# A two-layer diffusion backbone on one core: low parts of weights computed on POOL, modulation steps placed in other units

## The chip, the cores and the metric

The kernel runs on one core of a Trainium2 chip. The metric is the device time of one execution in microseconds (us); the median of 3 runs is 2028.29 us (2028.06 to 2028.62). Everything is float32, and the matmuls work on fp32r operands. The engines are TensorE (PE, with its weight loads as PEld), VectorE (DVE), ScalarE (ACT), GpSimd (POOL) and SyncE (SP), which issues most of the DMAs; POOL issues some.

## What is computed

Two layers over 256 latent tokens and 256 context tokens of width 1024. A vector of conditioning gives, per layer, nine modulation vectors of 1024 values for each of the two streams (`m`, from `w_ada`). A layer is a half-weighted SwiGLU FFN (hidden width 2816), a mixer with three branches (2-D Fourier, bidirectional retention, differential attention), and a second FFN. In the last layer only the latent stream goes on behind the mixer.

```python
m = (sc @ w_ada[l] + b_ada[l]).reshape(B, N_MOD, 1, D)
x = x + 0.5 * m[:, 2] * swiglu(modulate(rms_norm(x, norm_g[l, 0]), m[:, 0], m[:, 1]), w1[l, 0], w3[l, 0], w2[l, 0])
h = modulate(rms_norm(x, norm_g[l, 1]), m[:, 3], m[:, 4])
...
mixed = gf * (f_out @ wbf) + gr * (r_out @ wbr) + gd * (d_out @ wbd)   # gf, gr, gd: sigmoid(h @ w_gates)
x = x + m[:, 5] * (mixed @ wo)
x = x + 0.5 * m[:, 8] * swiglu(modulate(rms_norm(x, norm_g[l, 2]), m[:, 6], m[:, 7]), w1[l, 1], w3[l, 1], w2[l, 1])
```

## The kernel before

**Three products for one.** Every large product is computed as hi·hi + hi·lo + lo·hi: a weight block of 128 x 4 x 256 values is loaded (`wraw`), ACT casts it to fp32r (`whi`, line 330), and an engine subtracts (`wlo = wraw - whi`, line 331, in `split_act`). `split` takes the engine as an argument; the default is DVE. Only the first weights and the branch weights of the mixers name POOL.

**The stages.** There are four FFNs and two mixers, in the order first FFN, first mixer, second FFN (layer 0's other), third FFN (layer 1's first), second mixer, last FFN. The first three FFNs work on 512 columns (`ffn_both`), the last one on 256 (`ffn`). Each `ffn_both` runs one list of units through `pipeline`: four ordinary units, then sevens and downs. A seven (`seven`, seven units of 24 matmuls of 256 columns) computes the up and the gate product of 256 hidden channels with seven products of half-size blocks instead of eight; sums of weight blocks (`s1` to `s4`) and of quarters of the normed input (`Forms.fills`) feed it. A down unit (`down`, `chunk`) multiplies up to four 128-row blocks of `w2`, 24 matmuls of 512 columns. The list is two sevens, eight downs, four sevens, eight downs, three sevens, six downs; the last two channel blocks follow by themselves.

**What sets the order.** In `pipeline` PE, DVE and ACT take the order in which the program is written. Unit i's weights are prepared three units ahead (ACT's cast, then the low part), behind what unit i - 1 left to do at once (`now`: the residual of line 553, or the additions of line 771), and before its modulation steps and its matmuls. The modulation vectors are made in between on DVE: a vector is eight steps, and each step loads 512 KB of `w_ada` (SP) and adds it, scaled, to two accumulators (two instructions of line 242; 240 for the first step). A vector ends with eight small matmuls (line 258), a copy on DVE (263) and four transposes (266). Where the steps go is said by a unit's `cost`: `want` grows by cost times `scale`, which is steps over the sum of costs, and up to two steps are issued in front of the unit. Until the first eight are done the scale is at least 1, since the gate vector is needed for the residual.

```python
if i < len(units):
    want += units[i].cost * (max(scale, 1) if did < KD else scale)
    if units[i].cost:
        for _ in range(2):
            if did < min(total, int(want + 1e-6)) and not held[0] and step():
                did += 1
```

POOL and SP aren't bound to that order; POOL also issues the second half of the loads of `s1` and `s3` (line 737), which is added to the first half in flight and waits for it. The raw weights and the modulation loads share five buffers.

**The mixers.** The scheduler orders them. `merged` runs once for each branch: for each of four pairs of channel blocks two gate pieces of `w_in` (128x1024 each, `split` in line 1389), 24 matmuls each, and the branch's own product. The first two branches' merges are woven into the attention as fill, the third stands behind it. The first mixer works on 512 columns and makes three vectors, the second on 256 and makes one, during its third merge and output product.

Of the kernel before, what the change touches and what calls it, by code (L numbers as in the profile page):

```python
# [17 lines left out]
P = 128  # L18
# [61 lines left out]
def dit_kernel(ctx: ExitStack, tc: tile.TileContext, I: dict, out: bass.AP):  # L80
# [544 lines left out]

    def pipeline(units, fills, steps, total, made):

# [16 lines left out]
        with tc.manual_schedule(engines={eng.PE, eng.DVE, eng.Activation}):  # L644
            for i in range(len(units) + 1):
                prev = units[i - 1] if i else None
                if prev:
                    if prev.need is not None:
                        assert did >= prev.need, did
                        finish(True)  # L650
                    for f in prev.now:
                        f()
                while pi < min(len(units), i + 4):
                    while li < len(units) and (li <= pi or out + units[li].takes <= 3):
                        if units[li].load:
                            units[li].load()
                        out += units[li].takes
                        li += 1
                    units[pi].w = units[pi].prep()
                    out -= units[pi].gives  # L660
                    pi += 1
                if pi < len(units) and units[pi].first:
                    units[pi].first()
                for f in fills.get(i, ()):
                    f()
                finish()
                if prev:
                    for f in prev.end:
                        f()
                if i < len(units):  # L670
                    want += units[i].cost * (max(scale, 1) if did < KD else scale)
                    if units[i].cost:
                        for _ in range(2):

                            if did < min(total, int(want + 1e-6)) and not held[0] and step():
                                did += 1
                    units[i].mm(units[i].w)
# [4 lines left out]
    class Forms:  # L682


        def __init__(self, norm, spare, first):
# [9 lines left out]

            def whole(o, a, b):
                v.tensor_tensor(o, a.bitcast(F32), b.bitcast(F32), ALU.add)

            def neg(a, b):
                v.scalar_tensor_tensor(a, a, -1.0, b, op0=ALU.mult, op1=ALU.subtract)  # L700

            self.fills = {
                1: [lambda: whole(t[2], h22, l22), lambda: whole(t[0], h11, l11), lambda: whole(t[1], h12, l12)],
                2: [lambda: v.tensor_tensor(t[0], t[0], t[1], ALU.subtract),
                    lambda: v.tensor_tensor(t[1], t[2], t[1], ALU.subtract)],
                3: [lambda: split_act(z[0][:, 0], z[1][:, 0], t[0]), lambda: split_act(z[0][:, 2], z[1][:, 2], t[1])],
                4: [lambda: whole(t[1], h21, l21), lambda: neg(t[0], t[2]),
                    lambda: split_act(z[0][:, 1], z[1][:, 1], t[0])],
# [15 lines left out]
    def seven(fm, wa, wb, c0, fp, done, cost):  # L724
# [58 lines left out]
        def gate(h, by):  # L783
# [7 lines left out]
            Unit(part("c", fm.t1, True), whole("s1"), None, 0, 0, [keep("p5", "c")], cost=0),  # L791
            Unit(part("b", fm.t2), whole("s2"), None, 0, 1, [keep("w1", "b")], cost=1, first=summed("s2", "s1", "a11")),
            Unit(part("a", fm.b21, True), whole("a12"), raw("a12", wa, 1), 1, 0, [add("q1", "a")], [silu(0, "q1")], cost=cost),
# [6 lines left out]
    def ffn_both(l, f, norm, mods, then, first):  # L800
# [5 lines left out]
        with tc.tile_pool(name=f"ffn{l}{f}", bufs=1) as fp:  # L806
# [12 lines left out]

            def chunk(w, r, n, c0, acc, start, stop, xs, **more):  # L820
                x = {}
# [9 lines left out]

                return Unit(mm, lambda: split(x["w"], n, 2 * P), load, 1, 1, **more)

# [31 lines left out]
            def down(cg, r0, kt, last, need):  # L865
# [18 lines left out]
                for k in range(0, kt, 4):  # L884
                    n = min(4, kt - k)
                    more = {"cost": 0.25 * n}
                    if k + n == kt and need is None:
# [19 lines left out]
            for c0, c1 in ((2, 4), (4, 8), (8, 11)):  # L907
                g0 = 0 if c0 == 2 else c0
                for c in range(c0, c1):
                    units += seven(fm, w1, w3, c * 2 * P, fp, to(c - g0), 1 if first and c < 4 else 0.3)  # L910
                for cg in range(4 if c1 < KF // 2 else 3):
                    units += down(cg, 2 * g0, 2 * (c1 - g0), c1 == KF // 2, KD if first and g0 == 0 and cg < 2 else None)
            made = []
            with norm.done():
                pipeline(units, fm.fills, ada(mods, fp, made), KD * len(mods), made)
            for _ in to_residual(w2, 6, (g["hi"], g["lo"]), NTOK, gate, st, fp, weight_places, 16, then, (3,)):
# [105 lines left out]
    def mixer(l, nq, entry, mods, then):  # L1022
# [38 lines left out]
        with tc.tile_pool(name=f"mx{l}", bufs=1) as mp:  # L1061
# [319 lines left out]
            def merged(n, get, pool):  # L1381
# [4 lines left out]
                for d in range(0, KD, 2):  # L1386
                    acc = get("pg")
                    for c in range(2):
                        wt = split([rowsof(win, 4 * c, 4, O_GT + n * D + d * P, 256)], 4, 256)
                        for k in range(4):  # L1390
# [129 lines left out]
    entry = mixer_entry(0)  # L1520
    ffn_both(0, 0, after, [(0, m) for m in range(2, 5)], entry, True)
    load_mixer_consts()
# [3 lines left out]
    after = ffn_entry(0, 1, NTOK)  # L1526
    mixer(0, NTOK, entry, [(0, m) for m in (5, 6, 7)], after)
    load_bias(1)()
    entry = ffn_entry(1, 0, NTOK)
    ffn_both(0, 1, after, [(0, 8)] + [(1, m) for m in range(3)], entry, True)  # L1530
    after = mixer_entry(1)
    ffn_both(1, 0, entry, [(1, m) for m in range(3, 7)], after, False)
    entry = ffn_entry(1, 1, L)
    mixer(1, L, after, [(1, 7)], entry)
    ffn(1, 1, entry, [(1, 8)], Output())
# [22 lines left out]
```

## Time and profile before

| what | value |
|---|---|
| median of 3 runs | 2028.29 us (2028.06 to 2028.62) |
| profiled execution | 2025.39 us, span 2023.6 us |
| PE busy | 1931.0 us, 95% |
| PEld busy | 1729.6 us, 85% |
| DVE busy | 1599.2 us, 79% |
| ACT busy | 977.9 us, 48% |
| POOL busy | 129.4 us, 6% |
| mean granted clock of PE | 0.986 |

A busy PE is one with a matmul in its pipeline, so its idle time is what can be read from it. Stretches are given in us from the span's start: first FFN 46 to 393, first mixer to 816, second FFN to 1191, third to 1555, second mixer to 1837, last FFN to the end. A wait names the engine and line that came last.

### The profile page before, as it was taken

The numbers are of one execution on the slowest core, as the hardware profiler recorded it, in microseconds if no ns is written. First come the engines' busy times: TensorE is split into PE (matmuls) and PEld (weight loads), VectorE is DVE, ScalarE is ACT, GpSimd is POOL, SyncE is SP. The second block draws the span as 40 slices with busy tenths as digits, with TensorE's granted clock in tenths as the row PEclk, the third lists the DMA queues.
The fourth block names the chain that finished last, engine by engine and source line by source line (L and its number), as shares of the span: only waits on it lengthen the run. The fifth ranks groups of instructions, "written<-read, shape, count | busy, mean of one in ns | idle before, by whom it ended". The sixth has DMA issues, their size and how long they took to land. (4 is left out here: it accounts for less than half of the span.)

```text
span 2023.6 us, 32546 instructions
## 1 busy us (share of the span) xinstructions
PE 1931.0 (95%) x12959; PEld 1729.6 (85%) x12959; DVE 1599.2 (79%) x2365; ACT 977.9 (48%) x1487; POOL 129.4 (6%) x86
## 2 busy tenths in 40 slices
PE   7899999999999999989999999999999999889998
PEld 5789989897777678888998988889898988889998
DVE  6888868698788865797887878888788689898655
ACT  4433525464476434542543545345254768555444
POOL 2100100000000110110100000011000001110000
PEclk8999999999999999999999999999999999999999
DMA  9875854454322433665876465778644334475763
GB/s 318 211 222 157 221 170 121 137 174 132 107 65 87 162 109 119 153 171 182 215 213 166 125 159 154 209 186 233 177 141 117 107 91 144 125 248 178 238 193 110
DMA packets 283296, 331.24 MB, mean 164 GB/s; under 512 B 15664, under 2 KB 265096, under 8 KB 282888
## 3 DMA queue, kind: packets, MB, share of 16 engines
q1 hardware_dynamic: 254632, 300.84, 47.0%
q0 software_dynamic: 28512, 28.32, 9.4%
q8 instruction: 102, 1.67, 0.3%
q14 instruction: 50, 0.41, 0.1%
HBM read 325.97 MB, written 3.15 MB: 163 GB/s over the span
## 5 line engine op out<-in xcount | busy, mean ns | idle before, releaser
L330 ACT CAST whi<-wraw 128x1024 fp32r<-128x1024 f32 (+2 forms) x368 | 366.7, 1000 | 506.6 <-PE py L326 198.2
L331 DVE TENSOR_TENSOR wlo<-wraw,whi 128x1024 fp32r<-128x1024 f32 (+2 forms) x340 | 398.5, 1176 | 155.6 <-ACT whi L330 151.3
L242 DVE SCALAR_TENSOR_TENSOR aacc<-wada,cs,aacc 128x1024 f32<-128x1024 f32 x224 | 279.4, 1284 | 2.5 <-DMA wada<-w_ada 2.4
L763 PE MATMUL p<-hhi_f,whi 128*128 128x256 f32 x864 | 246.1, 285 | 23.5 <-DVE half L771 23.5
L763 PE MATMUL p<-hlo_f,whi 128*128 128x256 f32 x864 | 243.3, 282 | 0.0
L763 PE MATMUL p<-hhi_f,wlo 128*128 128x256 f32 x864 | 243.1, 281 | 0.0
L763 PE MATMUL p<-zone,whi 128*128 128x256 f32 x1296 | 230.9, 281 | 5.9 <-ACT half L768 5.2
L763 PEld LDWEIGHTS p<-zone,whi 128*128 128x128 f32 x1296 | 198.9, 190 | 7.8 <-ACT half L768 6.7
L325 PE MATMUL py<-ghi,whi 128*128 128x512 f32 x492 | 192.5, 391 | 0.7 <-DVE modT L268 0.7
L763 PEld LDWEIGHTS p<-hhi_f,whi 128*128 128x128 f32 x864 | 165.2, 191 | 31.8 <-DVE half L771 19.2
L327 PE MATMUL py<-ghi,wlo 128*128 128x512 f32 x492 | 191.5, 389 | 0.0
L326 PE MATMUL py<-glo,whi 128*128 128x512 f32 x492 | 191.4, 389 | 0.0
L763 PE MATMUL p<-zone,wlo 128*128 128x256 f32 x648 | 181.8, 281 | 0.0
L325 PE MATMUL p<-hhi_f,whi 128*128 128x256 f32 (+1 forms) x576 | 177.7, 309 | 2.3 <-DVE hhi_f L398 2.3
L327 PE MATMUL p<-hhi_f,wlo 128*128 128x256 f32 (+1 forms) x576 | 176.5, 307 | 3.0 <-DVE wlo L331 2.4
L326 PE MATMUL p<-hlo_f,whi 128*128 128x256 f32 (+1 forms) x576 | 177.0, 307 | 0.3
L763 PEld LDWEIGHTS p<-hhi_f,wlo 128*128 128x128 f32 x864 | 166.4, 193 | 0.0
L763 PEld LDWEIGHTS p<-hlo_f,whi 128*128 128x128 f32 x864 | 165.2, 191 | 0.3
L327 PE MATMUL pg<-hhi_m,wlo 128*128 128x512 f32 (+1 forms) x384 | 131.2, 342 | 5.8 <-DVE wlo L331 5.8
L325 PE MATMUL pg<-hhi_m,whi 128*128 128x512 f32 (+1 forms) x384 | 133.2, 347 | 3.5 <-ACT whi L330 2.5
L737 POOL DMA_DIRECT2D s<-ffn_w x54 | 72.2, 1337 | 905.3 <-DMA s<-ffn_w 412.8
L326 PE MATMUL pg<-hlo_m,whi 128*128 128x512 f32 (+1 forms) x384 | 130.1, 339 | 0.0
(367 smaller groups left out, 4447.1 us busy)
## 6 DMA issues: line engine op xcount, KB each, us to landing
wraw<-ffn_w SPq DMA_DIRECT2D x229, 512.0 KB, 4.4
wada<-w_ada SPq DMA_DIRECT2D x128, 512.0 KB, 4.1
wraw<-w_in SPq DMA_DIRECT2D x64, 512.0 KB, 3.6
s<-ffn_w SPq DMA_DIRECT2D x54, 512.0 KB, 5.3
s<-ffn_w POOLq DMA_DIRECT2D x54, 512.0 KB, 7.4
wraw<-w_out SPq DMA_DIRECT2D x16, 512.0 KB, 3.8
wada<-w_ada SPq DMA_DIRECT2D x30, 256.0 KB, 6.4
wraw<-w_in SPq DMA_DIRECT2D x16, 384.0 KB, 3.7
```

Of the source, the lines that this page charges most:

```text
L242: v.scalar_tensor_tensor(acc[:, t], w, cs[:, k, t:t + 1], acc[:, t], op0=ALU.mult, op1=ALU.add)
L325: te.matmul(o, a, xh, start=start, stop=False)
L326: te.matmul(o, a, xl, start=False, stop=False)
L327: te.matmul(o, b, xh, start=False, stop=stop)
L330: s.copy(hi, src)
L331: eng.tensor_tensor(lo, src, hi.bitcast(F32), ALU.subtract)
L737: gp.dma_start(t, rowsof(second[0], 4 * second[1], 4, c0, 2 * P), accum_op=ALU.add)
L763: te.matmul(om, wt[w][:, k, cm], form[f][:, k], start=(first and k == m == n == 0), stop=(k == 3 and m == 1 and n == 2), skip_group_check= ...
```

## The change

It names POOL for the low parts of the down units' weights and of gate pieces (all of them in the first mixer, the first of each pair in the second), and for two of the sums over quarters of the normed input. The cost of a full down unit goes from 1 to 1.6; of a seven's three paying units two go to 0 (from 0.3) and one from 1 to 0.6, but for the first two sevens of the first FFN. The rule of the first eight steps holds in the first FFN alone. The vectors are made one stage earlier: four in each of the first three FFNs, three in the first mixer, none in the second, one in the last FFN as before.

```diff
-    def pipeline(units, fills, steps, total, made):
+    def pipeline(units, fills, steps, total, made, first):
...
-                    want += units[i].cost * (max(scale, 1) if did < KD else scale)
+                    want += units[i].cost * (max(scale, 1) if first and did < KD else scale)
...
-            def whole(o, a, b):
-                v.tensor_tensor(o, a.bitcast(F32), b.bitcast(F32), ALU.add)
+            def whole(o, a, b, eng=v):
+                eng.tensor_tensor(o, a.bitcast(F32), b.bitcast(F32), ALU.add)
...
-                1: [lambda: whole(t[2], h22, l22), lambda: whole(t[0], h11, l11), lambda: whole(t[1], h12, l12)],
+                1: [lambda: whole(t[2], h22, l22, gp), lambda: whole(t[0], h11, l11), lambda: whole(t[1], h12, l12)],
...
-                4: [lambda: whole(t[1], h21, l21), lambda: neg(t[0], t[2]),
+                4: [lambda: whole(t[1], h21, l21, gp), lambda: neg(t[0], t[2]),
...
-            Unit(part("b", fm.t2), whole("s2"), None, 0, 1, [keep("w1", "b")], cost=1, first=summed("s2", "s1", "a11")),
+            Unit(part("b", fm.t2), whole("s2"), None, 0, 1, [keep("w1", "b")], cost=max(cost, 0.6), first=summed("s2", "s1", "a11")),
...
-            def chunk(w, r, n, c0, acc, start, stop, xs, **more):
+            def chunk(w, r, n, c0, acc, start, stop, xs, eng=v, **more):
...
-                return Unit(mm, lambda: split(x["w"], n, 2 * P), load, 1, 1, **more)
+                return Unit(mm, lambda: split(x["w"], n, 2 * P, eng=eng), load, 1, 1, **more)
...
-                    more = {"cost": 0.25 * n}
+                    more = {"cost": 0.4 * n, "eng": gp}
...
-                    units += seven(fm, w1, w3, c * 2 * P, fp, to(c - g0), 1 if first and c < 4 else 0.3)
+                    units += seven(fm, w1, w3, c * 2 * P, fp, to(c - g0), 1 if first and c < 4 else 0)
...
-                        wt = split([rowsof(win, 4 * c, 4, O_GT + n * D + d * P, 256)], 4, 256)
+                        wt = split([rowsof(win, 4 * c, 4, O_GT + n * D + d * P, 256)], 4, 256,
+                                   eng=gp if shared or c == 0 else v)
...
-    ffn_both(0, 0, after, [(0, m) for m in range(2, 5)], entry, True)
+    ffn_both(0, 0, after, [(0, m) for m in range(2, 6)], entry, True)
...
-    mixer(0, NTOK, entry, [(0, m) for m in (5, 6, 7)], after)
+    mixer(0, NTOK, entry, [(0, m) for m in (6, 7, 8)], after)
...
-    ffn_both(0, 1, after, [(0, 8)] + [(1, m) for m in range(3)], entry, True)
+    ffn_both(0, 1, after, [(1, m) for m in range(4)], entry, False)
...
-    ffn_both(1, 0, entry, [(1, m) for m in range(3, 7)], after, False)
+    ffn_both(1, 0, entry, [(1, m) for m in range(4, 8)], after, False)
...
-    mixer(1, L, after, [(1, 7)], entry)
+    mixer(1, L, after, [], entry)
```

Three places show what this moves. DVE in the first seven of the second FFN (`half` and `w` are the places to which the banks are added, `ft` and `half` also sums of weights), before:

```order
L331 TENSOR_TENSOR wlo<-ft,whi 128x1024
L331 TENSOR_TENSOR hlo_f_7317<-half_7774,hhi_f_7316 128x4x256
L240 TENSOR_SCALAR aacc<-wada,cs 128x1024 x2
L331 TENSOR_TENSOR wlo<-wraw,whi 128x1024
L242 SCALAR_TENSOR_TENSOR aacc<-wada,cs,aacc 128x1024 x2
L771 TENSOR_TENSOR half_7774<-p_7957,half_7774 128x512
L331 TENSOR_TENSOR wlo<-wraw,whi 128x1024
L242 SCALAR_TENSOR_TENSOR aacc<-wada,cs,aacc 128x1024 x2
L771 TENSOR_TENSOR half_7775<-p_7956,half_7775 128x512
```

and in the change:

```order
L331 TENSOR_TENSOR wlo<-ft,whi 128x1024
L331 TENSOR_TENSOR hlo_f_7363<-half_7820,hhi_f_7362 128x4x256
L331 TENSOR_TENSOR wlo<-wraw,whi 128x1024
L771 TENSOR_TENSOR half_7820<-p_8003,half_7820 128x512
L331 TENSOR_TENSOR wlo<-wraw,whi 128x1024
L771 TENSOR_TENSOR half_7821<-p_8002,half_7821 128x512
```

The modulation steps are gone from between the low parts and the additions; in the first two sevens two instructions of line 240 are left. DVE in the first down group of the same FFN, from its first steps on, before:

```order
L240 TENSOR_SCALAR aacc<-wada,cs 128x1024 x2
L242 SCALAR_TENSOR_TENSOR aacc<-wada,cs,aacc 128x1024 x2
L331 TENSOR_TENSOR wlo<-wraw,whi 128x1024
L263 COPY mrow<-pa_8_8563 128x512
L242 SCALAR_TENSOR_TENSOR aacc<-wada,cs,aacc 128x1024 x2
L268 TENSOR_TENSOR modT_117<-pa_8_8563,biasT_118 128x16
L190 TENSOR_SCALAR gmod_123<-modT_117 128x16
L553 SCALAR_TENSOR_TENSOR xT<-py,gmod_123,xT 128x256 x12
```

and in the change:

```order
L242 SCALAR_TENSOR_TENSOR aacc<-wada,cs,aacc 128x1024 x6
L553 SCALAR_TENSOR_TENSOR xT<-py,gmod_123,xT 128x256 x4
L242 SCALAR_TENSOR_TENSOR aacc<-wada,cs,aacc 128x1024 x4
L553 SCALAR_TENSOR_TENSOR xT<-py,gmod_123,xT 128x256 x4
L242 SCALAR_TENSOR_TENSOR aacc<-wada,cs,aacc 128x1024 x4
L331 TENSOR_TENSOR wlo<-wraw,whi 128x1024
L553 SCALAR_TENSOR_TENSOR xT<-py,gmod_123,xT 128x256 x4
```

The group gets nine steps instead of six, its low parts are gone from DVE, and the residuals of the first two output blocks no longer wait for the vector. POOL around the second down group of that FFN (`s` are the second halves of the loads of `s1` and `s3`), before, where no low part lies between the FFN's loads:

```order
L737 DMA s_9766<-ffn_w 128x4x256
L737 DMA s_9771<-ffn_w 128x4x256
L737 DMA s_9945<-ffn_w 128x4x256
L737 DMA s_9950<-ffn_w 128x4x256
L737 DMA s_10194<-ffn_w 128x4x256
L737 DMA s_10199<-ffn_w 128x4x256
```

and in the change:

```order
L737 DMA s_9778<-ffn_w 128x4x256
L737 DMA s_9783<-ffn_w 128x4x256
L737 DMA s_9991<-ffn_w 128x4x256
L737 DMA s_9996<-ffn_w 128x4x256
L331 TENSOR_TENSOR wlo<-wraw,whi 128x1024 x8
L737 DMA s_10236<-ffn_w 128x4x256
L737 DMA s_10241<-ffn_w 128x4x256
```

The eight low parts of the group stand behind the loads of the first two sevens that follow the group.

## Rows read from the trace of the kernel before

**Rows 1.** The page, part 1: each engine's busy time, share and instructions

```profile
PE 1931.0 (95%) x12959; PEld 1729.6 (85%) x12959; DVE 1599.2 (79%) x2365; ACT 977.9 (48%) x1487; POOL 129.4 (6%) x86
```

**Rows 2.** Windows: stretch, length, busy PE, PEld, DVE, ACT, POOL, clock, DMA share, GB/s

```profile
78.00:130.00 52.00, 43.62 (x342) 42.65 (x341) 49.19 (x70) 24.69 (x30) 5.77 (x4) 0.93 0.77 194
...
552.00:706.00 154.00, 147.54 (x705) 113.06 (x703) 129.60 (x242) 94.52 (x198) 15.34 (x8) 1.00 0.33 105
...
861.00:913.00 52.00, 43.24 (x340) 42.14 (x339) 46.28 (x45) 23.18 (x28) 4.43 (x3) 0.93 0.71 184
913.00:958.00 45.00, 44.64 (x203) 35.86 (x202) 32.69 (x40) 9.83 (x10) 0.00 (x0) 1.00 0.52 162
958.00:1042.00 84.00, 80.14 (x684) 78.49 (x683) 73.42 (x77) 43.21 (x51) 10.38 (x8) 1.00 0.84 213
...
1087.00:1153.00 66.00, 61.75 (x514) 60.70 (x511) 55.46 (x60) 30.64 (x39) 1.30 (x1) 0.97 0.50 140
...
1238.00:1282.00 44.00, 41.02 (x339) 40.59 (x338) 40.19 (x40) 23.75 (x28) 4.55 (x3) 0.96 0.70 172
...
1330.00:1410.00 80.00, 76.98 (x660) 75.25 (x660) 69.52 (x71) 41.46 (x51) 9.08 (x7) 1.00 0.84 215
...
1458.00:1517.00 59.00, 56.55 (x489) 55.76 (x486) 51.08 (x53) 29.07 (x36) 1.53 (x1) 1.00 0.48 142
...
1668.00:1760.00 92.00, 83.89 (x668) 77.52 (x668) 82.83 (x166) 68.91 (x137) 13.94 (x8) 1.00 0.44 136
1760.00:1796.00 36.00, 26.63 (x176) 23.07 (x176) 34.55 (x40) 13.79 (x20) 7.96 (x3) 0.91 0.67 215
```

**Rows 3.** Waits of PE over the whole span: total us, times, longest

```profile
PE p L763 <- DVE half L771: 23.5, 18, 3.4
PE pa L266 <- DVE mrow L263: 6.4, 6, 2.0
```

**Rows 4.** Windows of line 242 alone: stretch, length, DVE busy (count), clock, DMA

```profile
861.00:913.00 52.00, 12.37 (x10) 0.93 0.71 184
913.00:958.00 45.00, 12.37 (x10) 1.00 0.52 162
...
1238.00:1282.00 44.00, 4.94 (x4) 0.96 0.70 172
...
1760.00:1796.00 36.00, 17.21 (x14) 0.91 0.67 215
```

**Rows 5.** Groups of instructions by shape, DVE and then POOL: busy us, mean ns

```profile
L331 DVE TENSOR_TENSOR wlo<-wraw,whi 128x1024 fp32r<-128x1024 f32 x304 | 370.1, 1220 | 145.8 <-ACT whi L330 141.6 <-PE pf L1225 3.5
...
L242 DVE SCALAR_TENSOR_TENSOR aacc<-wada,cs,aacc 128x1024 f32<-128x1024 f32 x224 | 279.4, 1284 | 2.5 <-DMA wada<-w_ada 2.4
...
L553 DVE SCALAR_TENSOR_TENSOR xT<-py,gmod,xT 128x256 f32<-128x256 f32 x184 | 77.7, 476 | 51.4 <-PE py L327 51.2
...
L331 DVE TENSOR_TENSOR wlo<-wraw,whi 128x512 fp32r<-128x512 f32 x20 | 13.4, 685 | 3.0 <-ACT whi L330 2.9
...
L331 POOL TENSOR_TENSOR wlo<-wraw,whi 128x768 fp32r<-128x768 f32 x16 | 34.4, 2152 | 207.9 <-ACT whi L330 186.2 <-DVE sums L1332 16.8 <-DVE wlo L331 4.9
```

**Rows 6.** Timeline of DVE: start us, duration us, line, operation

```profile
717.89 1.27 DVE L242 SCALAR_TENSOR_TENSOR aacc<-wada,cs,aacc 128x1024 f32<-128x1024 f32 x1
...
719.69 2.87 DVE L242 SCALAR_TENSOR_TENSOR aacc<-wada,cs,aacc 128x1024 f32<-128x1024 f32 x1
...
1708.97 0.74 DVE L1413 SCALAR_TENSOR_TENSOR xT<-gt,pb 128x256 f32<-128x256 f32 x2
```

**Rows 7.** Timeline of POOL: start us, duration us, line, operation

```profile
15.67 4.65 POOL L331 TENSOR_TENSOR wlo<-wraw,whi 128x1024 fp32r<-128x1024 f32 x2 [15.22 <-ACT whi L330]
...
250.54 1.30 POOL L737 DMA_DIRECT2D s<-ffn_w  x1 [7.66 <-DVE wlo L331]
...
718.94 2.54 POOL L331 TENSOR_TENSOR wlo<-wraw,whi 128x768 fp32r<-128x768 f32 x1 [18.95 <-ACT whi L330]
...
1708.65 2.11 POOL L331 TENSOR_TENSOR wlo<-wraw,whi 128x768 fp32r<-128x768 f32 x1 [8.08 <-ACT whi L330]
```

More of the change, by code (lines that the diff above doesn't have):

```diff
@@ L914, in ffn_both @@
             with norm.done():
-                pipeline(units, fm.fills, ada(mods, fp, made), KD * len(mods), made)
+                pipeline(units, fm.fills, ada(mods, fp, made), KD * len(mods), made, first)
             for _ in to_residual(w2, 6, (g["hi"], g["lo"]), NTOK, gate, st, fp, weight_places, 16, then, (3,)):
```

## The prediction, made before the change was run

> **What bounds the kernel now.** The page first: PE is busy 1931.0 us, 95% of the span of 2023.6 us, DVE 79%, POOL 6% [rows 1]. Nearly all matmuls stay as they are, so a gain can only come out of the 92.6 us in which PE idles (2023.6 - 1931.0), and the windows tell where it does. The columns to compare are the length and PE's busy time: in the first two seven-product groups of the second FFN PE is idle 8.8 us of 52.0 with DVE busy 46.28, in the third branch merge of the second mixer 9.4 us of 36.0 with DVE busy 34.55; in the first down group of the second FFN only 0.4 us of 45.0 [rows 2]. PE's own waits name DVE: 23.5 us for line 771, which adds a seven's bank to its place in SBUF, and 6.4 us for the copy that ends a modulation vector [rows 3]. Line 771 stands on DVE behind whatever was queued before it, and that is where line 242 lies: 10 modulation instructions in 861 to 913 and 14 in 1760 to 1796, against 4 in the same piece of the third FFN, 1238 to 1282, where the same matmuls (339 against 340) fit into 44.0 us instead of 52.0 [rows 2, 4]. So the bound is DVE, late in a few stretches; elsewhere it is PE.
>
> **What moves, by the order.** Low parts: 19 of 128x1024 and 3 of 128x512 in each of three FFNs, two sums of a norm's quarter in each, 24 gate pieces in the first mixer and 12 in the second: 57 + 6 + 36 = 99 large instructions and 9 small ones leave DVE, where they take 1.220 and 0.685 us [rows 5]. The small ones are under a microsecond each and go with the rest. On POOL the only pair of that size took 4.65 us, 2.33 us each [rows 7]. Modulation: the vector of the second mixer leaves it, one more is made in the first FFN; each step is a load of 512 KB on SP and two instructions of line 242 (1.284 us, [rows 5]). SP gets the loads in groups with a DMA share of 0.52 instead of 0.71 [rows 2]; I put them at nothing. With the gate vector of the second FFN made earlier, its first residuals no longer wait for it, which frees PSUM sooner and costs nothing.
>
> **Sevens of the second FFN, first two: -8 us.** Twelve modulation instructions become two. The twin in the third FFN still has 4 of line 242 and takes 8.0 us less; the bounds are half of that, and 12 if the twin's remaining 3.0 us of PE idle go too and the clock (0.93 against 0.96) comes back.
>
> **Merge in the second mixer: -9 us.** 14 x 1.23 us (17.21 us, [rows 4]) leave a DVE that was busy 34.55 of 36.0 us. PE needs 26.63 us, and DVE keeps 17 us of work plus POOL's pieces. Bounds: -3, if PE then waits for ScalarE instead, to -12, all idle time and part of the clock of 0.91.
>
> **The other sevens of the second and third FFN: -6 us.** PE idles 3.9 + 4.3 + 3.0 + 3.0 + 2.5 = 16.7 us there (958 to 1042, 1087 to 1153, 1238 to 1282, 1330 to 1410, 1458 to 1517, [rows 2]). A seven loses about one step, 2.6 of some 20 us (four lie in the 80.0 us). Bounds 0 and -13; I take a third, because part of these are the ends of vectors.
>
> **The first FFN: +1 us.** Its first two sevens (8.4 us idle in 78 to 130, [rows 2]) keep their six steps: nothing. A fourth vector ends there; such an end costs PE 1.1 us of waiting (6.4 / 6, [rows 3]). Bounds 0 and 3.
>
> **Down units, what POOL costs: +2 us.** First what the rows show. A modulation instruction that ran beside a POOL low part took 2.87 us instead of 1.27 and ended at 722.56 us, 1.08 us after the piece (718.94 + 2.54); two instructions that read one operand from PSUM ran beside another POOL piece in 0.74 us, undisturbed [rows 6, 7]. So a POOL piece stops a DVE instruction that reads two operands from SBUF, and line 242 is one. The first down group of the second FFN then holds on DVE 32.69 us [rows 2], less five low parts (6.1), plus three more steps (7.7), plus up to five POOL pieces (11.7): 46.0 of 45.0 us. A lag of a few microseconds at its end is covered by the lookahead: units are prepared three ahead, some 5 us each (eight lie in the 45.0 us). PE itself now waits for POOL's low parts, which have the same three units. If the cover is gone, each of six groups costs up to 2 us: bounds 0 and +12. Queue: POOL's accumulating loads of the next two sevens now stand ahead of a group's low parts. The tightest was issued at 250.54 us before a group that begins at 256: 1.30 us, then 2.33 us, still in time [rows 7].
>
> The Trainium skill (SBUF — State Buffer, "SBUF: two separate sides") states this as a rule: the port pair that the two engines share is an exclusive lock, held for the whole instruction, and the loser blocks entirely. The rows agree for 2.87 against 1.27 us; by the rule each of the 99 pieces could cost DVE its full POOL time, and the sum would be that of the slower rival below.
>
> **Gates in the mixers: +4 and +2 us.** In the attention of the first mixer (552 to 706) 16 pieces leave DVE (-19.5 us) and may stop it for 16 x 2.33 = 37.3 us: 129.60 becomes up to 147.4 of 154.0 us, as much as PE's 147.54 [rows 2]. In the second (1668 to 1760) it is 8 pieces, 82.83 - 9.8 + 18.6 = 91.6 of 92.0. No row shows how often DVE is free or on PSUM then. At best DVE stands no more behind low parts that wait for ScalarE, and PE regains half its idle 6.5 and 8.1 us: -3 and -4. At worst every piece costs 1.11 us net and the delayed softmax nearly all of it: +16 and +9. I take the quarter nearer to nothing, since PE's idle time there is small and the scheduler places fill matmuls between.
>
> **Sum.** -8 - 9 - 6 + 1 + 2 + 4 + 2 = -14 us. The profiled execution took 2025.39 us, the median of the three runs is 2028.29, 2.9 us more; -14 on the median gives 2014.3, I say **2014**.
>
> **Rivals.** *Slower: POOL stops DVE.* Place: the attention stretches and the ends of the down groups. The mixers cost +16 and +9, the six groups +12, the first FFN +3; the gains shrink to -8 - 9 - 3: +20 us, about 2048. It decides from where DVE has less than 1.1 us free for each POOL piece. For it: 91.6 of 92.0 us above, and the 2.87 us instruction. Against: DVE as a whole goes from 1599 to at most 1599 - 121 + 231 = 1709 us, 84% of the span. The lock of the Trainium skill (SBUF — State Buffer, "SBUF: two separate sides") leads here if it binds every pair. *No change.* The sevens' gain holds only in part (-4, as PE then waits for ScalarE's copies), the merge gives -7, the others -2, and the mixers take +13 back: 2028. For it: the new low parts still wait for the same casts of ScalarE. *The change doesn't do what it says:* the group sums are still late because POOL's own quarter sum stands behind an accumulating load, so the first sevens gain nothing: 2022, inside the forecast's range and counted as a lesser gain.
>
> **How the numbers follow.** From no change a measurement here can tell about 0.2%, 4.1 us. The forecast (a gain of over 4.1 us, with the lesser gain) has 0.66; no change 0.18; slower 0.16. The likeliest case's own range is 2003 to 2024. Adding no change and the nearer part of slower gives 2002 to 2031, which leaves out under 2 in 10: a further gain if all bounds fell well, and the far side of the slow rival.
>
> **What would show it.** Right: line 242 at two instructions or fewer in the second FFN's first two sevens, and these about 44 us long; line 771's wait under 14 us in all; the merge of the second mixer under 29 us with no line 242 in it; DVE instructions of line 242 in down groups with a mean well over 1.3 us, and PE still under 1 us idle there. Wrong: a new wait of PE for POOL's low parts of more than 5 us, the wait for the softmax weights grown by over 10 us, or line 771 late at the first seven after each down group.

## The result and the profile after

The change takes **2055.81 us** (median of 3 runs, 2050.66 to 2059.64) against 2028.29; the ratio is 1.0133, 95% interval 1.0098 to 1.0169. It is slower by 27 us where 14 us less were forecast. The profiled execution took 2059.64 us, 34 more than that of before. Part 1 of its page answers to [rows 1]:

```profile
PE 1938.1 (94%) x12959; PEld 1731.2 (84%) x12959; DVE 1613.5 (78%) x2257; ACT 977.2 (47%) x1487; POOL 392.9 (19%) x194
```

DVE has 108 instructions fewer and is busy 14 us longer. The groups by shape show why (line 242 answers to [rows 5]; of the softmax line 1328, which subtracts in a tile of 128x2, before stands in the fence behind):

```profile
L242 DVE SCALAR_TENSOR_TENSOR aacc<-wada,cs,aacc 128x1024 f32<-128x1024 f32 x224 | 321.5, 1481 | 6.6 <-DMA wada<-w_ada 6.6
...
L331 POOL TENSOR_TENSOR wlo<-wraw,whi 128x1024 fp32r<-128x1024 f32 x97 | 251.5, 2676 | 672.0 <-ACT whi L330 667.6 <-DVE zone L1098 2.5 <-DVE z L981 1.8
...
L1328 DVE TENSOR_SCALAR nm<-nm 128x2 f32<-128x2 f32 x36 | 16.4, 455 | 0.4
```

```profile
L1328 DVE TENSOR_SCALAR nm<-nm 128x2 f32<-128x2 f32 x36 | 10.6, 295 | 0.2
```

The same 224 instructions of line 242 take 1481 ns each instead of 1284. The windows of after (columns of [rows 2]): the first two sevens of the first FFN, the attention of the first mixer, first sevens and first down group of the second FFN, its second down group, first sevens of the third FFN, its second down group; then attention and third merge of the second mixer:

```profile
79.00:141.00 62.00, 47.14 (x339) 46.01 (x338) 54.17 (x74) 26.38 (x33) 16.27 (x9) 0.86 0.73 182
576.00:731.00 155.00, 139.18 (x628) 105.54 (x628) 120.69 (x210) 86.87 (x184) 45.53 (x20) 0.94 0.24 74
...
911.00:952.00 41.00, 39.54 (x335) 39.10 (x334) 31.47 (x31) 23.75 (x28) 10.71 (x7) 1.00 0.74 171
952.00:997.00 45.00, 45.00 (x205) 36.36 (x204) 41.62 (x35) 9.39 (x9) 16.04 (x7) 1.00 0.58 186
...
1080.00:1129.00 49.00, 47.57 (x213) 37.24 (x212) 44.74 (x40) 9.64 (x10) 18.07 (x8) 1.00 0.66 196
...
1276.00:1317.00 41.00, 39.49 (x335) 39.01 (x334) 31.52 (x31) 23.73 (x28) 11.74 (x7) 1.00 0.74 176
...
1442.00:1490.00 48.00, 46.56 (x203) 36.10 (x202) 44.64 (x40) 9.21 (x9) 17.60 (x8) 1.00 0.66 195
...
1702.00:1800.00 98.00, 80.72 (x609) 75.16 (x608) 80.72 (x147) 65.05 (x131) 35.41 (x16) 0.95 0.39 123
1800.00:1835.00 35.00, 34.90 (x296) 33.40 (x295) 22.95 (x40) 21.97 (x34) 13.77 (x7) 1.00 0.57 180
```

The first sevens of the second FFN are 41 us long, and line 242 is gone from them (its own windows, answering to [rows 4]); the third merge is full of PE's work, 34.90 of 35.00. These gains are there. But the attention of the first mixer has 628 matmuls in 155 us where before had 705 in 154, with a granted clock of 0.94 instead of 1.00.

```profile
911.00:952.00 41.00, 0.00 (x0) 1.00 0.74 171
952.00:997.00 45.00, 25.65 (x14) 1.00 0.58 186
...
1800.00:1835.00 35.00, 0.00 (x0) 1.00 0.57 180
```

PE's waits, answering to [rows 3], with the softmax weights and POOL's low parts:

```profile
PE p L763 <- DVE half L771: 13.8, 7, 4.0
PE pa L266 <- DVE mrow L263: 12.2, 9, 3.0
PE pT L1343 <- DVE ex L1335: 10.4, 6, 2.3
...
PE pg L327 <- POOL wlo L331: 1.6, 2, 1.1
```

Line 771 fell from 23.5 to 13.8 us, as forecast. PE hardly waits for POOL itself (1.6 us). Where the time went is seen by cutting both traces at the same matmuls (from the first matmul of a stretch to the first of the next, us; the other columns are experiments):

| stretch | before | change | gates of first mixer alone | nothing on POOL | the same, three vectors in first FFN |
|---|---|---|---|---|---|
| first FFN, with the first mixer's projections | 473.7 | 497.3 | 479.2 | 485.2 | 472.2 |
| attention and merges of the first mixer | 218.7 | 243.5 | 241.8 | 219.3 | 218.5 |
| output product to the end of the second FFN | 467.4 | 456.5 | 466.5 | 452.6 | 452.5 |
| third FFN, with the second mixer's projections | 429.0 | 425.6 | 429.3 | 422.6 | 425.4 |
| attention and merges of the second mixer | 136.2 | 133.0 | 136.5 | 118.9 | 119.0 |
| rest | 213.9 | 216.7 | 219.9 | 214.8 | 216.2 |

Between before and the change: +24 in the first FFN, +25 in the first mixer, -11 and -3 in the second and third FFN, -3 in the second mixer. The last stretch, whose code is the same everywhere, differs by 6 us between runs, so differences below that are not read by themselves. Part of the +24 can be of this kind: the first two sevens of the first FFN took 55.8 us in the run of the third column and 51.1 before, though the two kernels are alike up to there.

**What a POOL piece does to DVE.** Timeline of DVE in the attention of after (start, duration), then ACT, then POOL:

```profile
670.82 0.47 DVE L1335 SCALAR_TENSOR_TENSOR ex<-ex,sums 128x256 f32<-128x256 f32 x1
671.21 2.36 DVE L1328 TENSOR_SCALAR nm<-nm 128x2 f32<-128x2 f32 x1
673.48 2.13 DVE L1149 CAST qk<-part 32x512 fp32r<-32x512 f32 x5
...
673.66 0.47 ACT L1330 ACTIVATE ex<-pD,nm 128x256 f32<-128x256 f32 x1 [1.57 <-DVE nm L1328]
...
670.90 2.65 POOL L331 TENSOR_TENSOR wlo<-wraw,whi 128x1024 fp32r<-128x1024 f32 x1 [5.20 <-ACT whi L330]
```

An instruction on two numbers per partition, which takes 0.16 us alone, ended with POOL's piece and took 2.36 us; ACT's exponential waited 1.57 us for it. Here PE had fill matmuls to do. Some 40 us earlier it had not (DVE, PE, POOL of after):

```profile
629.98 2.50 DVE L1149 CAST qk<-part 32x512 fp32r<-32x512 f32 x1
...
634.92 0.73 PE L1325 MATMUL pD<-qk 96*128 96x512 f32 x2 [1.76 <-DVE zone L1357]
...
629.57 2.63 POOL L331 TENSOR_TENSOR wlo<-wraw,whi 128x1024 fp32r<-128x1024 f32 x1 [2.51 <-ACT whi L330]
```

A cast that takes 0.42 us alone took 2.50, what stands behind it on DVE came 2 us later, and PE waited 1.76 us for the copy of line 1357 at its end; before, PE has no wait for line 1357 in the attention. The windows around it (columns of [rows 2]) show PE's clock:

```profile
620.00:634.00 14.00, 12.40 (x56) 8.68 (x54) 12.55 (x19) 10.15 (x19) 5.02 (x2) 1.00 0.15 39
634.00:640.00 6.00, 3.02 (x11) 2.17 (x12) 4.53 (x9) 3.19 (x8) 1.33 (x1) 0.66 0.35 105
640.00:646.00 6.00, 6.00 (x22) 4.82 (x21) 2.69 (x6) 1.83 (x6) 0.00 (x0) 0.77 0.15 52
646.00:660.00 14.00, 13.51 (x74) 10.64 (x74) 8.84 (x15) 8.90 (x20) 6.58 (x3) 1.00 0.24 69
```

PE idled 3 of 6 us, its granted clock fell to a mean of 0.66, and it was still 0.77 in the next 6 us, in which PE was busy throughout. (The second wait in the 6 us, 2.06 us, stands behind a POOL piece of 128x512 that before has as well.)

At the second down group of the second FFN, DVE and then POOL:

```profile
1080.72 0.69 DVE L786 SCALAR_TENSOR_TENSOR gt<-p,gt 128x512 f32<-128x512 f32 x1 [2.10 <-PE p L763]
1081.33 7.10 DVE L786 SCALAR_TENSOR_TENSOR gt<-half,gt 128x512 f32<-128x512 f32 x1
1089.54 1.22 DVE L331 TENSOR_TENSOR glo<-gt,ghi 128x1024 fp32r<-128x1024 f32 x1 [1.11 <-ACT ghi L330]
...
1077.11 1.30 POOL L737 DMA_DIRECT2D s<-ffn_w  x1 [7.72 <-issue]
1077.88 9.99 POOL L331 TENSOR_TENSOR wlo<-wraw,whi 128x1024 fp32r<-128x1024 f32 x4
```

POOL's queue stood behind an accumulating load, then four pieces ran without a gap. The instruction that reads a bank (`p`) took its 0.69 us beside them; the next one, with both operands in SBUF, was held for 7.10 us. PE then waited 1.4 us for what follows from it (ACT's cast `ghi` and DVE's low part `glo`).

### The profile page after: what moved, and what is told of

It reads as the page before. It is cut to its first block, busy times and chain, and to the rows that moved or that the text cites. A ratio compares the mean times of both kernels' runs of the same rounds, so it can differ in the third digit from the quotient of the medians.

```text
span 2057.8 us, 32621 instructions
## 1 busy us (share of the span) xinstructions
PE 1938.1 (94%) x12959; PEld 1731.2 (84%) x12959; DVE 1613.5 (78%) x2257; ACT 977.2 (47%) x1487; POOL 392.9 (19%) x194
## 4 chain that ended last, share of the span: by engine, by line
PE 70%; DVE 17%; ACT 6%; issue 4%; DMA 4%; SPq 0%; POOL 0%; DVEq 0%; ACTq 0%; POOLq 0%
PE p L763 21%; PE py L325 6%; PE py L326 6%; PE py L327 6%; DVE aacc L242 3%; PE p L326 3%; PE p L325 3%; PE p L327 3%; DVE wlo L331 2%; PE pj L326 2%; PE pj L325 2%; PE pj L327 2%; PE pg L326 2%; PE pg L327 2%; PE pg L325 2%
## 5 line engine op out<-in xcount | busy, mean ns | idle before, releaser
L331 POOL TENSOR_TENSOR wlo<-wraw,whi 128x1024 fp32r<-128x1024 f32 (+2 forms) x130 | 310.7, 2456 | 789.8 <-ACT whi L330 785.4
L331 DVE TENSOR_TENSOR wlo<-wraw,whi 128x1024 fp32r<-128x1024 f32 (+2 forms) x238 | 292.6, 1235 | 89.5 <-ACT whi L330 88.4
L242 DVE SCALAR_TENSOR_TENSOR aacc<-wada,cs,aacc 128x1024 f32<-128x1024 f32 x224 | 321.5, 1481 | 6.6 <-DMA wada<-w_ada 6.6
L763 PE MATMUL p<-hhi_f,whi 128*128 128x256 f32 x864 | 243.4, 282 | 13.8 <-DVE half L771 13.8
```

Of the source, the lines that this page charges most:

```text
L242: v.scalar_tensor_tensor(acc[:, t], w, cs[:, k, t:t + 1], acc[:, t], op0=ALU.mult, op1=ALU.add)
L331: eng.tensor_tensor(lo, src, hi.bitcast(F32), ALU.subtract)
L763: te.matmul(om, wt[w][:, k, cm], form[f][:, k], start=(first and k == m == n == 0), stop=(k == 3 and m == 1 and n == 2), skip_group_check= ...
```

## The experiments

**The parts, each undone or done alone.** Theory: POOL's pieces stop DVE. The edits, in this order: the gates of the first mixer back on DVE; before with those gates alone on POOL; the down units back on DVE; nothing new on POOL, so the placing of steps and vectors alone.

```diff
# gates1_dve, on the change
-   eng=gp if shared or c == 0 else v)
+   eng=gp if not shared and c == 0 else v)
# only_gates1, on before
-   O_GT + n * D + d * P, 256)], 4, 256)
+   O_GT + n * D + d * P, 256)], 4, 256, eng=gp if shared else v)
# downs_dve, on the change
-   more = {"cost": 0.4 * n, "eng": gp}
+   more = {"cost": 0.4 * n}
# no_pool, on the change: that of downs_dve, and
-   eng=gp if shared or c == 0 else v)
+   eng=v)
-   whole(t[2], h22, l22, gp)
+   whole(t[2], h22, l22)
-   whole(t[1], h21, l21, gp)
+   whole(t[1], h21, l21)
```

> The changed kernel, but the first mixer's gate low parts are on DVE again. Theory (POOL's low parts hold what DVE needs and stretch its small softmax operations): the first mixer's attention goes back from 267.8 us to 241 us, nothing else moves; 2056 - 27 = 2029 us. Rival (the mixer's 27 us come from the later start and the lower granted clock behind a slower first FFN): under 8 us come back, 2048 us or more.

> The kernel before, with one part of the change alone: the first mixer's gate low parts on POOL. Theory: the same 27 us in the attention stretch, 2028 + 27 = 2055 us. Rival (the loss needs the other parts, as a POOL that is late from the FFN or the new order of vectors in the mixer): under 8 us, 2036 us or less.

> The changed kernel, but the down units' low parts are on DVE again. Theory (POOL's pieces stop line 242 and the sums of the FFNs, and stand between the accumulating loads): the first FFN gets back at least 12 of its 21 us, the second down groups of the second and third FFN 4 us each; 2056 - 20 = 2036 us. Rival (the first FFN's loss is that of its fourth vector and of the two quarter sums on POOL): the first FFN gets back under 5 us, and DVE with nine steps and its own low parts in a down group is late by more; 2050 us or more.

> The changed kernel with nothing new on POOL: down units, gates of both mixers and the two quarter sums are on DVE; the placing of the modulation steps and the vectors stays. Theory: the FFNs' and the third merge's gains stay (-10, -9, -11 us) and the first FFN pays a fourth vector, 0 to 4 us; 2028 - 28 = 2000 us, range 1994 to 2008. Rival (the placing of the steps costs as much as POOL does, since a down group then has nine steps and its own low parts on DVE): down groups of the second and third FFN longer by 4 us or more each, 2015 us or more.

Measured, against before: gates1_dve 1.0015 [0.9998, 1.0031]; only_gates1 1.0144 [1.0116, 1.0172]; downs_dve 1.0071 [1.0050, 1.0092]; no_pool 0.9861 [0.9840, 0.9882], 1999.88 us. The gates of the first mixer cost 24 us in the change (1.0133 - 1.0015) and 29 us alone; the start of the mixer and the other parts have no say in it. Without POOL the rest of the change is worth 28 us, as the theory said. One point of it failed: the first FFN stays long, 485.2 us in the table. downs_dve missed too: 2044.32 us lies between its theory (2036) and its rival (2050 or more). The second down groups of the second and third FFN got back 3 us each (48.2 to 45.2 and 48.5 to 45.3) where 4 were expected; the first FFN got back 10 us (487.3), of which 5 are in its first two sevens, where kernels that are alike differ by as much.

**Lock, order or lateness.** The scheduler had also chosen another order once the low parts left DVE. So POOL's instruction was exchanged under an order that is the same but for three rows: by fills, which write without reading, and by four smaller pieces.

```diff
# both on only_gates1, in the gates of the first mixer alone
-   eng.tensor_tensor(lo, src, hi.bitcast(F32), ALU.subtract)
# gates1_fill
+   [gp.memset(lo.bitcast(F32), 0.0) for _ in range(2)]
# gates1_pieces
+   [gp.tensor_tensor(lo[:, i], src[:, i], hi[:, i].bitcast(F32), ALU.subtract) for i in range(4)]
```

> The kernel before with the first mixer's 24 gate low parts replaced by two fills of the same tile with zeros on POOL (the low part of these weights is left out of the product). PE, DVE and ACT keep the order of the run with the subtracts on POOL, but for 3 rows. Theory (a POOL instruction that reads SBUF stops DVE): POOL writes alone and stops little; DVE's small operations in the attention have their old durations, the attention is 220 to 228 us long, 2028 to 2035 us. Rival (the order that the scheduler chose when the low parts left DVE): the same loss, 2050 to 2060 us. Rival (any POOL instruction stops DVE, in proportion to its time): by half if the fills take half of 2.4 us, 2040 to 2048 us.

> The kernel before with the first mixer's gate low parts on POOL, each in four instructions of 128x256 in place of one of 128x1024; the order on PE, DVE and ACT is the same. Theory, if DVE gets its turn between two POOL instructions: the longest stop falls from 2.4 to some 0.7 us, half of the 24 to 30 us comes back, 2040 to 2046 us. Theory, if POOL's next instruction takes its turn first: the stops stay as long as four pieces together, 2055 to 2062 us. Rival (PE waits for POOL's low parts themselves, which come late): four instructions take longer than one, 2058 us or more, with the wait of PE for POOL above 10 us.

Measured: gates1_fill 0.9989 [0.9976, 1.0002], gates1_pieces 1.0042 [1.0029, 1.0056]. The windows of attention and merges: before, only_gates1, gates1_fill, gates1_pieces (columns of [rows 2]).

```profile
552.00:771.00 219.00, 211.26 (x983) 163.54 (x982) 170.09 (x289) 119.66 (x228) 21.57 (x11) 1.00 0.33 105
```

```profile
558.00:800.00 242.00, 219.16 (x983) 167.38 (x982) 175.25 (x267) 119.06 (x228) 73.64 (x32) 0.97 0.30 94
```

```profile
552.00:770.00 218.00, 211.25 (x984) 163.81 (x983) 146.81 (x268) 119.39 (x228) 59.35 (x53) 1.00 0.33 105
```

```profile
553.00:784.00 231.00, 215.40 (x983) 165.08 (x982) 160.86 (x267) 119.02 (x228) 92.22 (x95) 0.99 0.31 99
```

The third number with its count is DVE's. The same 267 instructions take 175.25 us beside POOL's subtracts and 146.81 beside fills: 28.4 us are lost to 21 new pieces (32 - 11), 1.35 us each. The order is not the cause, since fill and subtract share it. POOL's busy time is not either: the pieces are busy longest (92.22 us) and cost half of the stretch's loss (12 us against 23; 9 against 29 of the whole kernel), so DVE gets in between some of them. Lateness of the low parts is out for the pieces and for only_gates1, since PE waits next to nothing for POOL; fills stand earlier than subtracts, as they wait for no cast, and by themselves would not exclude it. Of the 23 us in only_gates1, 15.1 are idle time of PE (242.00 - 219.16 against 219.00 - 211.26) and 7.9 are longer matmuls: the same 983 take 219.16 us instead of 211.26, at a granted clock of 0.97 instead of 1.00. The windows above show the same in the change: the clock fell where PE had begun to wait.

**Where it costs.** Two placements in no_pool: one vector moved out of the first FFN, and the gates of the third merges alone on POOL.

```diff
# no_pool_3, on no_pool
-   [(0, m) for m in range(2, 6)], entry, True)
+   [(0, m) for m in range(2, 5)], entry, True)
-   [(0, m) for m in (6, 7, 8)], after)
+   [(0, m) for m in (5, 6, 7, 8)], after)
# third_only, on no_pool
-   eng=v)
+   eng=gp if n == 2 else v)
```

> The change without anything new on POOL and with three vectors in the first FFN, four in the first mixer. The first FFN was 11 us longer with a fourth vector than before even without POOL. Theory (the fourth vector's eight steps and its end are what it pays for): the first FFN gets 8 us or more back and the first mixer, where DVE is 84% busy in the attention but PE idles 6.5 us only, pays 2 to 6 us; 1994 us, range 1990 to 1998. Rival (DVE in the mixer has no room for 8 more steps, 20 us): the mixer pays 10 us or more, 2000 us or more.

> The change without anything new on POOL but for the gate low parts of the third merge in both mixers, 16 pieces, where no attention is left. Theory (it is the place: POOL's pieces cost where small DVE operations stand between two steps of PE): within 4 us of 2000 us, the run without POOL. Rival (each piece on POOL costs about 1 us anywhere, as 24 pieces cost 24 to 30 us in the first mixer): 2012 to 2018 us.

Measured: no_pool_3 0.9805 [0.9784, 0.9826], **1991.20 us**: faster than both kernels. third_only 0.9915 [0.9893, 0.9936]: 11 us over no_pool, so the rival has the size right and the theory failed as it stood. By the cut of the table 7.5 us of it lie in the first mixer (226.8 against 219.3) and 6.0 in the second (124.9 against 118.9). But it is not a price per piece, and the pieces were not all where no attention is left: in the first mixer the low parts are made ahead, and four of the eight ran before 735, beside the last heads. Windows of the first mixer's third merge in third_only, its beginning and its rest:

```profile
735.00:750.00 15.00, 11.64 (x40) 9.03 (x39) 5.62 (x5) 5.83 (x6) 4.75 (x2) 0.77 0.20 61
750.00:789.00 39.00, 38.73 (x175) 30.48 (x174) 17.58 (x21) 14.37 (x18) 8.75 (x4) 1.00 0.35 104
```

In the rest two gate pieces and two that no_pool has as well go with 0.3 us of idle PE. At the beginning ACT's cast of the third branch, and the gate's tanh behind it, wait for the norms of the last heads on DVE (two of their instructions took 3.50 us at 724.23 beside a piece, 1.41 in no_pool), and PE, which then runs at the lower of its two levels (1.2 and 2.4 GHz) for a while, waits for both:

```profile
735.76 0.39 PE L327 MATMUL pg<-hhi_m,wlo 128*128 128x512 f32 x1
739.51 0.80 PE L325 MATMUL pb<-half,whi 128*128 128x512 f32 x1 [3.35 <-ACT gt L1402]
740.10 0.63 PE L326 MATMUL pb<-half,whi 128*128 128x512 f32 x1
```

In no_pool the same wait was 1.30 us and the matmuls behind it took 0.39. How much of this is the held norms, and how much the order of 30 matmuls that the scheduler changed, is not separated, and the second mixer's 6.0 us are not followed up. Moving a vector gave the first FFN its time back (472.2 us), and the mixer took eight more steps for nothing (218.5). The last three sevens of the first FFN, no_pool and then no_pool_3:

```profile
308.00:372.00 64.00, 60.44 (x508) 59.80 (x507) 52.58 (x56) 31.45 (x38) 1.30 (x1) 1.00 0.51 138
```

```profile
302.00:362.00 60.00, 59.34 (x517) 58.13 (x516) 43.53 (x48) 31.93 (x39) 1.88 (x2) 1.00 0.42 110
```

Eight instructions of line 242 (56 - 48) are 4 us there; the other 9 us of the 13 are spread over the rest of the first FFN.

**The other parts alone, and the fill once more.** Each on no_pool.

```diff
# downs_gp
-   more = {"cost": 0.4 * n}
+   more = {"cost": 0.4 * n, "eng": gp}
# downs_fill: as downs_gp, each subtract replaced by two fills of wlo
# sums_gp
-   whole(t[2], h22, l22)
+   whole(t[2], h22, l22, gp)
-   whole(t[1], h21, l21)
+   whole(t[1], h21, l21, gp)
# gates2_gp
-   eng=v)
+   eng=gp if not shared and c == 0 else v)
```

> The change without anything new on POOL, but for the down units' low parts, which are on POOL. Theory (POOL's subtracts stop the residuals' and line 242's instructions and the sums of the next seven): the first FFN 5 us longer than in the run without POOL, the second down groups of the second and third FFN 2 to 3 us each; 2000 + 10 = 2010 us, range 2004 to 2014. Rival (POOL costs in the mixers alone): 2002 us or less.

> As the run with the down units' low parts on POOL, with two fills of the same tile in place of each subtract (the low part of w2 is left out of the product); the order on PE, DVE and ACT is the same. Theory (what costs is a POOL instruction that reads SBUF beside DVE): back to the run without POOL less the DVE time that was saved, 1994 to 2002 us. Rival (POOL's queue: the low parts stand behind accumulating loads and come late): a fill stands in the same queue behind the same loads, 2005 us or more.

> The change without anything new on POOL, but for the two sums over quarters of the normed input per FFN, which are on POOL. Theory: two instructions of 2.9 us per FFN that stop a DVE addition each, 1 to 2 us in each of three FFNs: 2000 + 4 = 2004 us. Rival (they are hidden by the fills behind them): 2001 us or less.

> The change without anything new on POOL, but for the first gate piece of each pair in the second mixer. Theory (as in the first mixer, about 1 us for each of 12 pieces and more where the softmax chain has no slack): the mixer's stretch of 119 us gets 12 to 17 us longer, 2014 us. Rival (the loss in the second mixer was POOL being late from the down units): under 5 us, 2005 us or less.

Measured: downs_gp 0.9915 [0.9888, 0.9942], downs_fill 0.9843 [0.9805, 0.9882], sums_gp 0.9876 [0.9845, 0.9907], gates2_gp 0.9939 [0.9916, 0.9961]. So the down units cost 11 us and nothing with fills in the same queue behind the same loads: there too it is the read, and the queue only heaps up the pieces. Where the 11 us lie is shown in part: the second down group of the third FFN takes 48.9 us against 45.3 in no_pool, that of the second 46.5 against 45.3, and in the change both take 3 us more. The profiled execution of downs_gp took 2003.88 us, 3 more than that of no_pool, so it can't place the rest. The sums' 3 us lie within the intervals. The second mixer's gates cost 16 us; the 14 that the profiles show are all in its attention. That stretch and the third merge in no_pool:

```profile
1659.00:1743.50 84.50, 76.40 (x612) 70.94 (x611) 76.93 (x153) 65.39 (x132) 13.86 (x8) 1.00 0.45 139
1743.50:1777.70 34.20, 34.12 (x291) 32.78 (x289) 23.34 (x43) 21.88 (x32) 5.97 (x4) 1.00 0.59 183
```

In gates2_gp they take 98.5 and 34.5 us, in the change 98 and 35: the pieces in this third merge cost nothing. The parts add up: -28 for the placing, +29, +16, +11 and +3 for POOL make +31; the change measured +27, with an interval of 7 us either way and each part's of some 5.

## Why the prediction was wrong

- **First sevens of the second FFN, -8:** right, 51.3 to 41.2 us, line 242 gone. The bound of -12 held.
- **Third merge of the second mixer, -9:** the mechanism was right, the size was not. From the last matmul of the second merge to its end it takes 34.3 us in no_pool (1743.4 to 1777.7), and took 51.4 before (1752.0 to 1803.4). Line 242 is busy for 17.21 us in it [rows 4], but the gain is made of two parts: PE's idle time goes from 9.4 us to 0.1, and its busy time from 42.03 us (303 matmuls at a granted clock of 0.93) to 34.22 (291 at 1.00; 12 fewer, those of a vector's end). The first part is what I read; the second is the term that I mis-sized, under 3 us of "part of the clock" where busy time gave 7.8. The premise that a gain can only come out of the 92.6 us of idle time left it out: in no_pool as a whole PE's idle time fell by 16 us and its busy time by 9 (1931.0 to 1922.1).
- **Other sevens, -6:** in no_pool the five groups gave 14 us, just past the bound of -13.
- **First FFN, +1, bounds 0 and 3:** wrong. I priced the end of a vector and left out its eight steps. They go into an FFN whose last three sevens had PE busy 60.92 of 61 us before (300 to 361); sixteen instructions more on DVE make nearly every group of it longer. Placing alone costs 11 to 13 us (485.2 against 473.7 and 472.2). The change takes 12 more, 9.3 of them in the first two sevens (61.6 us against 52.3). How much of that is POOL is open: a small load (`lv`) that DVE waits for at the first seven was late by 0 to 4.39 us in kernels that are alike up to there, 2.81 in the change and 1.30 in no_pool.
- **Down units, +2, bounds 0 and +12:** 11. The step that failed was that three units of lookahead cover a late DVE. It covers the low parts, but the sums and the silu product of the last seven stand on DVE in front of PE's next operand, and a row of four pieces holds them for 7 us. That is shown for the second down groups of the change, 3 us each in the second and third FFN; the rest of the 11 is not placed. The first down group, which I had worked out, lost nothing (45.00 us busy of 45.00).
- **Gates, +4 and +2, bounds to +16 and +9:** 24 to 29 and 16. This is the failure that decides the sign, and it lies in one sentence: "I take the quarter nearer to nothing, since PE's idle time there is small and the scheduler places fill matmuls between." The rows gave the price (the held instruction of [rows 6] lost 1.60 us, 2.87 - 1.27; measured 1.35 per piece), and I weighed it against DVE's free time as a sum. The sum did stay small: in only_gates1 DVE was busy 5 us more than before in that stretch (175.25 against 170.09), in 242 us, and 18.4 of 20 us where it was fullest; the kernel lost 23 us there. What counted was that a tiny instruction of a chain that runs from DVE to ACT to PE waits out a whole piece, and PE with it; and that a PE that waits runs at a lower clock afterwards (0.66 and 0.77 in the windows above), which no bound held. Small idle time of PE before said only that the chain was just in time. Two smaller errors: the bound counted 16 of the first mixer's 24 pieces; and the rule that a piece stops an instruction "that reads two operands from SBUF" was too narrow, since line 1328 and the cast of line 1149 read one and were held all the same. [rows 7] shows one of two such pairs on POOL; the other, at 40.92, took 5.60 us, so 2.33 us was the shorter price.

Together the placing was forecast at -22 us (-8 - 9 - 6 + 1) and measured at -28 in no_pool. That these are near is partly luck: the sevens gave 10 us more, the merge 8 more, and the first FFN took 10 more.

The slower rival named the right mechanism and the right places, at 2048 us; its point of decision (DVE with less than 1.1 us free for each piece) was the wrong one, as DVE had room. The signs named beforehand did not tell the cases apart. Those of being right nearly all came: no line 242 in the first sevens of the second FFN, these 41 us long, line 771 at 13.8 us, line 242 in the first down group at 1.83 us (25.65 / 14) with PE never idle. Those of being wrong hardly did: PE waited 1.6 us for POOL's low parts in the mixers and 0.6 elsewhere, not over 5; the softmax wait of line 1335 grew from 5.4 to 10.4 us, not by over 10, since PE's waits in the attention are spread over many lines; and line 771 was late by 1.0 to 1.5 us at the first seven after three of the down groups, as it is in no_pool. And still the kernel was 27 us slower.

The Trainium skill (SBUF — State Buffer, "SBUF: two separate sides") gives the lock for a DVE operation with two SBUF inputs only against a POOL operation that reads SBUF, and for DVE's two-port mode against any. The trace agrees on the first, and on the second if the one-operand instruction below runs in that mode, which no row names. In gates1_fill, DVE and then POOL:

```profile
594.00 1.17 DVE L1334 TENSOR_SCALAR ex<-ex,sums 128x256 f32<-128x256 f32 x1
595.20 0.48 DVE L1335 SCALAR_TENSOR_TENSOR ex<-ex,sums 128x256 f32<-128x256 f32 x1
...
594.07 2.00 POOL L1389 MEMSET wlo<- 128x1024 f32 x2 [5.76 <-PE pg L327]
```

Beside fills the two-input instruction takes its usual 0.48 us, while the one-input instruction, 0.35 us alone, is held until the first fill ends (594.07 + 2.00 / 2 = 595.07). Weighing that sentence by the sum of DVE's free time was the mistake, not the sentence.

## What to carry to other kernels

Before work is moved from DVE to POOL, look for short DVE instructions that stand between two steps of PE, and count one whole POOL piece for each that can meet one; DVE's share of busy time said nothing on that here. Where POOL has to work beside such a chain, the cheaper ways are those tried here: fills cost nothing, pieces of a quarter of the size a third to a half of what whole ones cost, and pieces in a stretch without such a chain (the second mixer's third merge in gates2_gp) nothing. Moving work in time on the same engine, out of the stretches in which that engine is late, gave the whole gain here; but a stretch in which the bounding engine is fully busy pays for what it is given, even if the other engine has room.

## What the runs showed of the hardware that was not expected

- Back to back POOL subtracts leave DVE no turn between them: 7.10 us for an instruction of 0.68. In pieces of 128x256 DVE does get some turns: the longest instruction of line 1328 took 1.62 us instead of 2.37 in only_gates1, and the loss of DVE time 14.1 us (160.86 - 146.81) instead of 28.4, though POOL was busy 18.6 us longer (92.22 - 73.64).
- About half of the 97 subtracts of 128x1024 on POOL take 2.35 to 2.5 us. The mean of 2.68 holds rows of several, whose records overlap (four of some 2.9 us in 9.99 us), so it does not show what POOL itself loses beside DVE. A fill of that size takes 0.98 us.
